# Layer 1's parts in another order, a softmax factor moved behind the product with the values, low parts of weights in pieces, and page arithmetic made earlier

## The chip, the core and the metric

The kernel runs on one core of a Trainium2 chip. The metric is the device time of one execution in microseconds (us), the median of several executions. Five engines of the core matter. TensorE (PE) multiplies; its operands are loaded by PEld rows. VectorE (DVE), ScalarE (ACT) and GpSimd (POOL) work on tiles. SyncE (SP), ACT's queue and POOL's queue issue DMA transfers. Each engine executes its own instructions in program order and waits for others by semaphores.

## What is computed

One inference step of a decoder with two layers, for a prompt of 512 tokens and 8 x 4 sample tokens, with the same weights. All matrices are float32; the width is 1024.

```python
for layer in range(DEPTH):
    hp = rms_norm(xp, norm_mix[layer])                 # and hs for the samples
    if layer % 2 == 0:                                 # HGRN2: gated linear recurrence, 6 heads
        tp, sp = hgrn2_mixer(hp @ w_in_hgrn, ...)
    else:                                              # DSA: 6 query heads, 2 key/value heads
        qp, kp, vp, iqp, ikp, iwp = dsa_project(hp @ w_in_dsa, ...)
        tp = dsa_prompt(qp, kp, vp, iqp, ikp, iwp)     # 128 keys chosen for each query by an index score
        ts = dsa_sample(...)                           # 256 of 1028, keys and values read by a page table
    cp = memory_attention(zp[..., -MEM_WIDTH:], ...)   # 4 heads into 256 memory tokens
    xp = xp + concat([tp, cp]) @ w_out[layer]
    xp = xp + conv_ffn(rms_norm(xp, norm_ffn[layer]), ...)

def gathered_attention(q, kg, vg, valid):
    s = einsum('btgrd,btkgd->btgrk', qg, kg) * D ** -0.5
    p = softmax(where(valid, s, -inf))                 # exp(s - max) / sum
    return einsum('btgrk,btkgd->btgrd', p, vg)
```

The outputs are the residual streams of both groups, the recurrent states, and the new keys and values.

## The kernel before

Activations lie feature-major, 128 features by 544 tokens (32 samples, then 512 prompt tokens). Every weight product is made of float32r parts: a weight block of 128x1024 (a unit) is loaded into raw, ACT casts it into whi, and DVE or POOL makes wlo = raw - whi; activations are split in hi and lo in the same way. A product is then three matmuls for each block: hi by whi, lo by whi, hi by wlo. 199 units are used in a fixed order.

The program is written out by a planner in Python. A main stream emits the products in order; beside it a Pump holds generators, each of which emits a few instructions of a head, a choice of keys or an attention per step and says on which tiles the step waits. A Model keeps a rough clock for each engine, and a step is given out when that clock says that its tiles are ready. Priorities (PRI, smaller first) and limits (KEEP, MAIN0, MAIN1, SLACK, BUSY, URGENT, MARGIN) decide among the steps. MIX orders the parts of layer 0: a number is a head of HGRN2 (its f and q products), hi two of its value products, g a gate product, mem the memory keys and values. ORDER does the same for layer 1: index (keys and queries of the index), q (one query head each), k, v, mq (memory queries), mkv, attn (which adds the attention's generators). All instructions are issued through one helper (L398 in the trace), so rows are told apart by tile names.

What the change and the prediction touch:

- Weights._cut (L740 to L762) casts a unit and makes its low part. The engine is chosen on the planner's clocks: DVE, if its clock is not later than that of PE and POOL plus a lead. The lead is LEAD0 = -1 in layer 0 and the MLPs, and LEAD1 = -100 in layer 1, so that there every low part goes to POOL, as one instruction of 1024 columns, about 21 of them.
- The page arithmetic (L1578 to L1592) stands after the output projection of layer 0: nine DMAs on ACT's queue load the page table in two forms (ptb, ptv), and DVE makes addresses of it (iidx, vidx). The next things on DVE are the sums and the factor of the following norm (tiles m__finish and rs), which PE spreads over the partitions (rb__finish).
- proj_tm makes a token-major product; for the samples it adds hi and lo of the 32 sample columns (eight POOL adds into sam) at each call, five calls in all.
- choose_sample finds the 256th largest score of a sample token bit by bit. A digit is a chain on DVE, ACT and PE: small integer instructions of 128x7 set seven thresholds, three counts of 128x264 run on DVE and four on ACT, and PE sums them (tile ple_choose_sample). One digit goes with one q product in the order of the program.
- choose_prompt takes the 128 largest scores of a query tile in 16 rounds; a round is MAX8 and MATCH_REPLACE8 on 256, 384 or 512 columns of isc. sbias and isc then mask the scores.
- prompt_attn (L1940) goes, for each head and query tile, from the scores (as) through exp (p, with its row sum su) to the transposes (apt, pt) and the product with the values (ao). scale_rows(p, su) multiplies p by 1/su on DVE or ACT before the transposes. In the last product the values are stationary, so ao is feature-major and is copied to outs[hd]; joined(hd) splits all 544 columns of it when the samples are there too.
- out_proj takes the heads in the order LAST.

```python
late = max(model.t["pe"], model.t["pool"]) + self.lead
(V if model.t["dve"] <= late else G).tensor_sub(lo[:, c:c + n], raw[:, c:c + n], hi[:, c:c + n].bitcast(F32))
```

## Time and profile before

| | |
|---|---|
| median of 3 runs | 1513.89 us (1504.01, 1513.89, 1514.38) |
| the profiled execution's span | 1500.7 us, mean granted clock 0.978 |
| PE busy | 1434.9 us (96%), 11314 matmuls |
| PEld, DVE, ACT, POOL busy | 1345.6, 803.2, 587.5, 567.3 us |
| DMA | 152.5 MB, mean 102 GB/s |
| chain that ended last | PE 84%, DVE 11%, issue 2%, ACT 1%, DMA 1% |

A share of busy time is a mean over stages with different limits; the granted clock is that of PE, 1.00 being its full rate. Layer 0's mixer runs to about 286 us, its output projection to 340, its MLP to 748; layer 1's mixer from 748 to 1049, then its output projection and MLP to the end. In a row of the timeline the bracket tells how long the engine was idle before the instruction, and what ended that idle time.

### The profile page before, as it was taken

How to read it: one execution, taken by the hardware profiler on the slowest of the kernel's cores; microseconds unless marked ns; L12 is line 12 of the kernel's file. 1: busy time of each engine (PE TensorE's matmuls, PEld its weight loads, DVE VectorE, ACT ScalarE, POOL GpSimd, SP SyncE). 2: the span in 40 equal slices, each digit the busy share in tenths (PEclk: the TensorE clock that was granted, in tenths of full speed). 3: DMA queues.
4: the chain of work that ended last, by engine and by line, in shares of the span. 5: the costliest groups of instructions: out<-in, count | busy, mean ns of one | idle time of the engine just before them, and what ended most of it. 6: DMA issues, size and time to landing. Idle time of an engine off the chain costs nothing.

```text
span 1500.7 us, 28191 instructions
## 1 busy us (share of the span) xinstructions
PE 1434.9 (96%) x11314; PEld 1345.6 (90%) x11314; DVE 803.2 (54%) x1762; ACT 587.5 (39%) x1064; POOL 567.3 (38%) x600
## 2 busy tenths in 40 slices
PE   8989999998999999999999797689999999999998
PEld 7978889998999999999987775456999999999998
DVE  7466886653444234444469988867444442244431
ACT  5447466332333123333335443466333331133320
POOL 4422444323444124446753444341134440144410
PEclk9999999999999999999999997989999999999999
DMA  5542132321333223224414236631222323232241
GB/s 186 177 156 64 59 117 86 101 85 62 88 95 93 92 73 94 90 85 126 135 54 131 83 115 202 199 127 57 71 76 89 96 85 99 73 95 87 85 121 57
DMA packets 60145, 152.52 MB, mean 102 GB/s; under 512 B 9040, under 2 KB 22960, under 8 KB 60016
## 3 DMA queue, kind: packets, MB, share of 16 engines
q1 hardware_dynamic: 39456, 110.11, 23.9%
q0 software_dynamic: 8208, 26.50, 5.4%
q10 hardware_dynamic: 12352, 14.13, 2.9%
q8 instruction: 89, 1.46, 0.4%
q14 instruction: 40, 0.33, 0.1%
HBM read 142.23 MB, written 8.47 MB: 100 GB/s over the span
## 4 chain that ended last, share of the span: by engine, by line
PE 84%; DVE 11%; issue 2%; ACT 1%; DMA 1%; another core or an unknown queue 0%; ACTq 0%; POOL 0%; SPq 0%; DVEq 0%; POOLq 0%
PE a L398 71%; DVE ple_choose_sample L398 2%; PE u_hgrn_head L398 1%; DVE isc_index_prompt L398 1%; PE id_index_prompt L398 1%; PE mkv L398 1%; PE ao_prompt_attn L398 1%; PE ho_hgrn_head L398 1%; PE ms_prompt L398 1%; PE hgrn_head_samples L398 1%; PE as_prompt_attn L398 1%; DVE t L398 1%; DMA ptv<-pt 1%; DVE lo L398 1%; PE mo_prompt L398 1%
## 5 line engine op out<-in xcount | busy, mean ns | idle before, releaser
L398 PE MATMUL a<-hi,whi 128*128 128x272 f32 x2640 | 556.4, 292 | 1.4 <-DVE t L398 1.0
L398 PE MATMUL a<-lo,whi 128*128 128x272 f32 x2640 | 551.0, 290 | 4.9 <-DVE lo L398 4.6
L398 POOL TENSOR_TENSOR wlo<-raw,whi 128x1024 fp32r<-128x1024 f32 x143 | 342.7, 2397 | 557.3 <-ACT whi L398 551.1
L398 PE MATMUL a<-hi,wlo 128*128 128x272 f32 x2640 | 549.1, 289 | 0.0
L398 PEld LDWEIGHTS a<-hi,whi 128*128 128x128 f32 x2640 | 417.7, 190 | 9.2 <-issue 5.4
L398 PEld LDWEIGHTS a<-lo,whi 128*128 128x128 f32 x2640 | 418.1, 190 | 6.2 <-DVE lo L398 5.6
L398 PEld LDWEIGHTS a<-hi,wlo 128*128 128x128 f32 x2640 | 418.1, 190 | 0.0
L398 ACT ACTIVATE whi<-raw 128x1024 fp32r<-128x1024 f32 (+1 forms) x202 | 209.5, 1038 | 230.9 <-PE a L398 151.3
L398 DVE TENSOR_TENSOR wlo<-raw,whi 128x1024 fp32r<-128x1024 f32 (+1 forms) x59 | 79.7, 1351 | 160.6 <-ACT whi L398 157.7
L398 DVE TENSOR_TENSOR sc<-a,rb 128x544 f32<-128x544 f32 x53 | 38.4, 724 | 116.1 <-PE a L398 114.5
L398 DVE SCALAR_TENSOR_TENSOR conv<-ext,params,conv 128x560 f32<-128x560 f32 x88 | 70.6, 802 | 45.1 <-ACT conv L398 43.6
L398 DVE TENSOR_TENSOR ext<-a,rb 128x240 f32<-128x240 f32 x132 | 37.5, 339 | 105.9 <-PE a L398 102.2
L398 ACT ACTIVATE conv<-ext,params 128x560 f32<-128x560 f32 x44 | 37.6, 855 | 136.2 <-DVE ext L398 132.6
L398 ACT ACTIVATE hi<-sc 128x544 fp32r<-128x544 f32 x44 | 29.0, 658 | 137.3 <-DVE sc L398 137.3
L398 DVE TENSOR_TENSOR x<-a,x 128x544 f32<-128x544 f32 x48 | 34.7, 723 | 80.1 <-PE a L398 72.5
L398 POOL TENSOR_TENSOR sqa<-sqa,sq 128x544 f32<-128x544 f32 x24 | 34.8, 1448 | 110.0 <-ACT sq L398 108.3
L398 DVE TENSOR_TENSOR sc<-sc,conv 128x512 f32<-128x512 f32 x88 | 62.5, 748 | 4.9 <-DVE sc L398 0.5
L398 ACT ACTIVATE conv<-conv 128x560 f32<-128x560 f32 x44 | 29.6, 672 | 73.8 <-DVE conv L398 73.8
L398 ACT ACTIVATE hi<-x,params 128x544 fp32r<-128x544 f32 x32 | 23.9, 745 | 70.4 <-DVE x L398 68.5
L398 DVE TENSOR_TENSOR lo<-sc,hi 128x544 fp32r<-128x544 f32 x44 | 31.9, 725 | 31.9 <-ACT hi L398 31.9
L398 PE MATMUL a<-whi,hi 128*128 128x256 f32 x160 | 46.8, 293 | 0.0
L398 PE MATMUL a<-whi,lo 128*128 128x256 f32 x160 | 45.1, 282 | 0.0
(406 smaller groups left out, 1931.9 us busy)
## 6 DMA issues: line engine op xcount, KB each, us to landing
raw<-w SPq DMA_DIRECT2D x177, 512.0 KB, 3.6
raw<-w POOLq DMA_DIRECT2D x21, 512.0 KB
k_sample_scores<-ckT SPq DMA_DIRECT2D x46, 128.0 KB, 3.5
ck_mem_samples<-cmkT ACTq DMA_DIRECT2D x16, 256.0 KB, 6.2
cv_mem_samples<-cmv ACTq DMA_DIRECT2D x16, 256.0 KB, 4.7
st_s<-hgrn_head_samples POOLq DMA_DIRECT2D x12, 256.0 KB
hgrn_head_samples<-hst SPq DMA_DIRECT2D x10, 256.0 KB, 3.5
ck_sample_scores<-ckT SPq DMA_DIRECT2D x18, 128.0 KB, 2.1
```

Source lines behind the costliest of these rows:

```text
L398: return f(*args, **kw)
```

## The change

It has six parts.

1. Order: MIX, ORDER and all of PRI, KEEP, MAIN0, MAIN1, SLACK, BUSY, URGENT, WAIT, MARGIN and PACE have other values, and the planner's costs know of PE's change between tile shapes and of the port that DVE and POOL share.
2. Low parts in layer 1: LEAD1 is -1, and what goes to POOL there is cut in pieces of 256 columns. By the order of the instructions, of the 21 low parts of this stage 12 are now on DVE and 9 on POOL, in four pieces each.
3. The factor 1/su is applied by ACT's copy of ao, no longer to p. So that it is a factor of rows, pt is now stationary, and ao comes out token-major; four transposes a head (aot) and a split bring it back. joined then splits only 32 sample columns. The samples' factor moves in the same way to their outputs.
4. Page arithmetic: the nine loads are issued before layer 0's heads, the addresses are made before its output projection.
5. sam is made once a layer (samples_of): 16 small POOL adds in place of 40.
6. Comments are gone.

```diff
-KEEP, MAIN0, MAIN1 = 3, 5, 1
+KEEP, MAIN0, MAIN1 = 0, 1, 5
-LEAD0, LEAD1, POOLED = -1.0, -100.0, 0
-WAIT, URGENT, EARLY = 1, 0.4, 0.4
+LEAD0, LEAD1, POOLED = -1.0, -1.0, 0
+PIECE = 256
+WAIT, URGENT, EARLY = 0, 0.2, 0.4
-PRI = dict(qsc=2, ip=2, isa=3, keys=3, sc=4, qsq=7, attn=5, sat=0, ...)
+PRI = dict(qsc=7.7, ip=5.5, isa=5.9, keys=7.5, sc=7.9, qsq=7.9, attn=6, sat=4.1, ...)
-MIX = "0 hi hi mem 1 2 3 4 hi 5 g g g g g g".split()
-ORDER = "index mem v q q q mem q q mem q k attn mq mkv".split()
+MIX = "0 hi hi mem g 1 2 3 4 g 5 hi g g g g".split()
+ORDER = "index q mem q mem q q q q k v mem attn mq mkv".split()
...
-                (V if model.t["dve"] <= late else G).tensor_sub(lo[:, c:c + n], raw[:, c:c + n], hi[:, c:c + n].bitcast(F32))
+                on, step = (V, n) if model.t["dve"] <= late else (G, self.piece)
+                for at in range(c, c + n, step):
+                    on.tensor_sub(lo[:, at:at + step], raw[:, at:at + step], hi[:, at:at + step].bitcast(F32))
...
+    ptb = cp.tile([128, 64], I32, name="ptb")
+    S.dma_start(ptb, bass.AP(tensor=pt_ap.tensor, offset=pt_ap.offset, ap=[[0, 128], [1, 64]]))
+    ptv = cp.tile([128, 8], I32, name="ptv")
+    for s in range(8):
+        S.dma_start(ptv[16 * s:16 * s + 16, :], bass.AP(tensor=pt_ap.tensor, offset=pt_ap.offset + s, ap=[[0, 16], [8, 8]]))
     memraw = []
...
-            scale_rows(p[:, :n], su)
-            yield [p]
...
-                T.matmul(ob[:, 0:128], vtok[k // 2][:, 256 * (k % 2) + 128 * g:256 * (k % 2) + 128 * g + 128],
-                         pt[:, 128 * k:128 * k + 128], start=k == 0, stop=k == tq)
-            S.activation(outs[hd][:, NS + 128 * tq:NS + 128 * tq + 128], ob[:, 0:128], AF.Copy)
+                T.matmul(ob[:, 0:128], pt[:, 128 * k:128 * k + 128],
+                         vtok[k // 2][:, 256 * (k % 2) + 128 * g:256 * (k % 2) + 128 * g + 128],
+                         start=k == 0, stop=k == tq)
+            S.activation(ot[:, 128 * tq:128 * tq + 128], ob[:, 0:128], AF.Copy, scale=su)
+        yield [ot]
+        tb = bank("aot")
+        for tq in range(4):
+            T.transpose(tb[:, 128 * tq:128 * tq + 128], ot[:, 128 * tq:128 * tq + 128], ident)
+        cat[hd] = pair()
+        yield from split2(tb, cat[hd], slice(NS, NT))
...
-        scale_rows(p, ri)
...
+        V.tensor_scalar(o[:, :256], o[:, :256], ri, None, op0=ALU.mult)
         yield [o]
```

Where the instructions now stand is decided by the planner. The first place is DVE's queue around the page arithmetic; before, it stands between the last square sum of the output projection (sqa) and the chain of the next norm's factor (m__finish).

```order
L398 TENSOR_TENSOR sqa_3520<-sqa_3520,sq_4038 128x544
L398 TENSOR_SCALAR iidx<-ptb,consts_81 64x32 x2
L398 TENSOR_SCALAR vidx<-ptv,consts_81 128x8
L398 TENSOR_SCALAR vidx<-vidx 128x8 x3
L398 TENSOR_SCALAR m__finish_1_4120<-st__finish_1_4111 128x5
L398 TENSOR_SCALAR m__finish_2_4122<-m__finish_1_4120 128x5
L398 TENSOR_SCALAR rs_4066<-m__finish_2_4122 128x5
```

In the changed kernel it stands between the last products of layer 0's heads (sc, on) and the split of a gated head (lo_gate):

```order
L404 TENSOR_TENSOR sc_3319<-sc_3319,on_hgrn_head_1_3447 128x544
L404 TENSOR_TENSOR sc_3474<-a_3328,rb_310 128x544
L404 TENSOR_SCALAR iidx<-ptb,consts_81 64x32 x2
L404 TENSOR_SCALAR vidx<-ptv,consts_81 128x8
L404 TENSOR_SCALAR vidx<-vidx 128x8 x3
L404 TENSOR_TENSOR lo_gate_1_3517<-sc_3319,hi_gate_1_3516 128x544
L404 TENSOR_SCALAR m_hgrn_head_2_3527<-m_hgrn_head_1_3028 128x5
```

The wait for ptv has moved ahead of the output projection, to a place where ptv was issued long before, and no longer stands ahead of m__finish.

The second place is DVE's queue in one q product of layer 1, before. rq and t are the rotation of a query head, ple_choose_sample (here by its longer names, _sample_choose_sample) is one digit.

```order
L398 SCALAR_TENSOR_TENSOR rq_9394<-a_9265,params_79,tab_9116 128x544
L398 SCALAR_TENSOR_TENSOR t_6_9395<-a_9265,params_79,tab_9118 64x544 x2
L398 TENSOR_SCALAR _sample_choose_sample_2_9032<-_sample_choose_sample_3_9440,_sample_choose_sample_2_9032 128x7
L398 TENSOR_SCALAR _sample_choose_sample_1_9031<-_sample_choose_sample_2_9032 128x1
L398 TENSOR_TENSOR _sample_choose_sample_1_9031<-_sample_choose_sample_1_9031 128x7
L398 TENSOR_TENSOR _sample_choose_sample_1_9031<-_sample_choose_sample_1_9031 128x1
L398 TENSOR_TENSOR _sample_choose_sample_1_9031<-consts_81,_sample_choose_sample_1_9031 128x7
L398 TENSOR_SCALAR _sample_choose_sample_1_9036,_sample_choose_sample_4_9034<-row_index_sample_3_9027,_sample_choose_sample_1_9031,_sample_choose_sample_2_9032 128x264 x3
```

The same place in the changed kernel; the whole of raw, whi and wlo is one weight unit:

```order
L404 SCALAR_TENSOR_TENSOR rq_9350<-a_9281,params_79,tab_8742 128x544
L404 SCALAR_TENSOR_TENSOR t_7_9351<-a_9281,params_79,tab_8744 64x544 x2
L404 TENSOR_TENSOR wlo_9357<-raw_8750,whi_9356 128x1024
L404 TENSOR_SCALAR _sample_choose_sample_2_9152<-_sample_choose_sample_3_9387,_sample_choose_sample_2_9152 128x7
L404 TENSOR_SCALAR _sample_choose_sample_1_9151<-_sample_choose_sample_2_9152 128x1
L404 TENSOR_TENSOR _sample_choose_sample_1_9151<-_sample_choose_sample_1_9151 128x7
L404 TENSOR_TENSOR _sample_choose_sample_1_9151<-_sample_choose_sample_1_9151 128x1
L404 TENSOR_TENSOR _sample_choose_sample_1_9151<-consts_81,_sample_choose_sample_1_9151 128x7
L404 TENSOR_SCALAR _sample_choose_sample_1_9156,_sample_choose_sample_4_9154<-row_index_sample_3_9146,_sample_choose_sample_1_9151,_sample_choose_sample_2_9152 128x264 x3
```

A low part of 1024 columns has come in between the rotation and the digit. On POOL, where before each q product had an rq add, a wlo and a load, there are now only the rq add and the load. Counted in the same rows, 23 rounds of the prompt's choice (MATCH_REPLACE) stand ahead of sbias before, and 12 in the changed kernel; the last round of the last tile is row 1178 of DVE's queue before and row 1160 now. The first q product now stands ahead of the first digit.

The third place is PE's queue at the end of the attention, before: the last heads' products with the values, and the first products of the output projection (a, with a joined head).

```order
L398 MATMUL ao_prompt_attn_4_12176<-pt_prompt_attn_4_12157,v_9113 128x128 x2
L398 MATMUL apt_prompt_attn_4_12186<-consts_80,p_prompt_attn_4_12064 128x128 x4
L398 MATMUL ao_prompt_attn_4_12193<-pt_prompt_attn_4_12174,v_9110 128x128 x2
L398 MATMUL ao_prompt_attn_4_12193<-pt_prompt_attn_4_12174,v_9113 128x128 x2
L398 MATMUL mpt_prompt_3_12203<-consts_80,mp_prompt_2_11996 128x128 x4
L398 MATMUL ao_prompt_attn_4_12210<-pt_prompt_attn_4_12191,v_9110 128x128 x2
L398 MATMUL ao_prompt_attn_4_12210<-pt_prompt_attn_4_12191,v_9113 128x128 x2
L398 MATMUL mot_join_1_12220<-consts_80,mo_mem_samples_1_10771 128x128 x4
L398 MATMUL mo_prompt_1_12226<-mpt_prompt_2_11985,mv_11194 64x256 x2
L398 MATMUL mo_prompt_1_12226<-mpt_prompt_4_12208,mv_11194 64x256 x2
L398 MATMUL a_11327<-hi_joined_1_12200,whi_10839 128x272 x2
```

In the changed kernel (hi_prompt is the memory attention's part of the input, hi_prompt_attn a head's):

```order
L404 MATMUL ao_prompt_attn_4_12218<-v_10259,pt_prompt_attn_4_12203 128x128 x2
L404 MATMUL ao_prompt_attn_4_12218<-v_10262,pt_prompt_attn_4_12203 128x128 x2
L404 MATMUL apt_prompt_attn_3_12225<-consts_80,p_prompt_attn_3_12184 128x128 x3
L404 MATMUL a_11363<-hi_prompt_1_11753,whi_11079 128x272 x2
L404 MATMUL a_11363<-lo_prompt_1_11754,whi_11079 128x272 x2
L404 MATMUL a_11363<-hi_prompt_1_11753,wlo_11080 128x272 x2
L404 MATMUL aot_prompt_attn_1_12237<-consts_80,ct_prompt_attn_1_10871 128x128 x4
L404 MATMUL ao_prompt_attn_3_12245<-v_10259,pt_prompt_attn_3_12229 128x128 x2
L404 MATMUL ao_prompt_attn_3_12245<-v_10262,pt_prompt_attn_3_12229 128x128
L404 MATMUL as_prompt_attn_4_12250<-kT_9880,rq_9600 128x512
L404 MATMUL a_11362<-hi_prompt_attn_1_12030,whi_11079 128x272 x2
```

Products of the output projection now stand between the last heads' parts, and each head has its transposes (aot) behind its product with the values.

## Rows read from the trace of the kernel before

**Rows 1.** The page: its first line.
```profile
span 1500.7 us, 28191 instructions
```

**Rows 2.** Windows: from:to, length, busy us (instructions) of PE, PEld, DVE, ACT, POOL; clock, DMA.
```profile
1200.00:1300.00 100.00, 100.00 (x799) 100.00 (x799) 31.49 (x43) 23.93 (x26) 23.69 (x22) 1.00 0.31 91
```

**Rows 3.** Windows, the same columns, of the stages of layer 1.
```profile
748.00:778.00 30.00, 26.38 (x213) 25.67 (x214) 23.80 (x56) 6.25 (x9) 19.08 (x23) 0.99 0.22 65
778.00:870.00 92.00, 82.58 (x580) 70.20 (x580) 79.76 (x190) 50.02 (x129) 37.85 (x47) 0.95 0.29 90
870.00:912.00 42.00, 37.12 (x319) 32.06 (x318) 35.05 (x125) 20.77 (x49) 22.39 (x31) 0.94 0.49 151
912.00:976.00 64.00, 44.05 (x309) 28.57 (x309) 52.57 (x182) 25.09 (x72) 23.54 (x22) 0.82 0.64 205
976.00:1049.00 73.00, 67.05 (x441) 42.86 (x441) 51.95 (x156) 48.04 (x138) 22.83 (x24) 0.91 0.28 93
```

**Rows 4.** Timeline of DVE (start, duration, instruction, [idle before <-releaser]), 336 to 358.
```profile
349.65 0.23 DVE L398 TENSOR_SCALAR vidx<-ptv,consts 128x8 int32<-128x8 int32 x1 [10.00 <-DMA ptv<-pt]
...
352.35 0.17 DVE L398 SCALAR_TENSOR_TENSOR rs<-m__finish,rs 128x5 f32<-128x5 f32 x1
```

**Rows 5.** Timeline of PE, 338 to 354: the sums and the factor.
```profile
339.41 1.12 PE L398 MATMUL st__finish<-consts,sqa 128*128 128x1 f32 x16
...
352.57 1.36 PE L398 MATMUL rb__finish<-consts,rs 128*128 128x128 f32 x5 [5.05 <-DVE rs L398]
```

**Rows 6.** Windows, columns as above, after the wait.
```profile
353.00:359.00 6.00, 6.00 (x33) 5.54 (x32) 3.53 (x7) 2.21 (x4) 0.32 (x2) 0.64 0.00 0
```

**Rows 7.** Timeline of ACT and its queue (ACTq), 20 to 36 and 336 to 342.
```profile
33.79 0.69 ACT L398 ACTIVATE rb<-rb__finish 128x512 f32<-128x512 f32 x2 [5.24 <-PE rb__finish L398]
...
336.76 3.35 ACTq L398 DMA_DIRECT2D ptv<-pt  x7
```

**Rows 8.** Timeline of PE, 84 to 104: waits for a head.
```profile
90.27 0.63 PE L398 MATMUL ot_hgrn_head<-consts,o_hgrn_head 128*128 128x128 f32 x4 [1.50 <-DVE o_hgrn_head L398]
92.47 0.41 PE L398 MATMUL ots_hgrn_head<-consts,oss_hgrn_head 128*128 128x32 f32 x2 [1.57 <-DVE oss_hgrn_head L398]
```

**Rows 9.** Groups of POOL, 748 to 1049: sample columns.
```profile
L398 POOL TENSOR_TENSOR sam<-hi,lo 128x32 f32<-128x32 f32 x16 | 4.2, 296 | 0.1
```

**Rows 10.** Timeline of POOL, 846 to 862: one q product.
```profile
856.49 1.35 POOL L398 TENSOR_TENSOR rq<-rq,t 128x544 f32<-128x544 f32 x1 [7.92 <-DVE t L398]
857.81 2.38 POOL L398 TENSOR_TENSOR wlo<-raw,whi 128x1024 fp32r<-128x1024 f32 x1
```

**Rows 11.** Timeline of DVE, 846 to 866: the same q product.
```profile
850.95 0.17 DVE L398 TENSOR_TENSOR ple_choose_sample<-consts,ple_choose_sample 128x7 int32<-128x7 int32 x1
...
856.88 1.05 DVE L398 TENSOR_TENSOR ple_choose_sample<-ple_choose_sample 128x7 int32<-128x7 int32 x2
857.97 2.25 DVE L398 TENSOR_TENSOR ple_choose_sample<-consts,ple_choose_sample 128x7 int32<-128x7 int32 x1
...
864.65 1.02 DVE L398 TENSOR_TENSOR ple_choose_sample<-ple_choose_sample 128x7 int32<-128x7 int32 x2
```

**Rows 12.** Tile wlo, DVE, 1100 to 1500: count, ns min/median/max, first and last start.
```profile
L398 DVE TENSOR_TENSOR wlo<-raw,whi x14: 1224/1226/1227, 1238.8 to 1479.6; 128x1024 fp32r<-128x1024 f32 x14
```

**Rows 13.** Groups of DVE by shape, 748 to 1049: count, busy us, mean ns, idle before.
```profile
L398 DVE MATCH_REPLACE8 isc_index_prompt<-mpt_choose_prompt,isc_index_prompt 128x384 f32<-128x384 f32 x16 | 8.7, 543 | 0.0
...
L398 DVE TENSOR_SCALAR qss<-qss 128x30 f32<-128x30 f32 x2 | 3.0, 1518 | 0.0
```

**Rows 14.** The same, shapes together, and one of them in the timeline.
```profile
L398 DVE TENSOR_SCALAR p_prompt_attn<-p_prompt_attn,m_prompt_attn 128x512 f32<-128x512 f32 (+3 forms) x14 | 10.2, 726 | 0.5
...
962.86 3.18 DVE L398 TENSOR_SCALAR p_prompt_attn<-p_prompt_attn,m_prompt_attn 128x256 f32<-128x256 f32 x1
```

**Rows 15.** Timeline of PE, 966 to 1036: transposes of p, last scores.
```profile
971.29 0.60 PE L398 MATMUL apt_prompt_attn<-consts,p_prompt_attn 128*128 128x128 f32 x4
...
1030.30 5.42 PE L398 MATMUL as_prompt_attn<-kT,rq 128*128 128x512 f32 x12
```

81 lines of the change are left out of this document (46 added, 35 removed).

## Prediction

> **What bounds the kernel now.** I read the time in three steps: the page for the whole, the windows for the stages in which TensorE (PE) loses time, then the timelines of those stages for what it waits on. The profiled execution spans 1500.7 us [rows 1]. PE is the bound: over most of the program it is busy for the whole of a window at a granted clock of 1.00, as from 1200 to 1300, where 799 matmuls of a product take 100 us, 0.125 us each [rows 2]. There nothing in this change can help, since the products stay. So I count lost time: a stage's idle time plus its busy time x (1 - clock). In layer 1's mixer that is 3.9 us (748 to 778, index), 13.5 (778 to 870, scores, selection, q products), 7.1 (870 to 912), 27.9 (912 to 976, memory keys and first heads) and 12.0 (976 to 1049, the other heads), together 64 us of 301 [rows 3]. From 778 to 912 it is VectorE (DVE) that is busy, 79.8 of 92 and 35.1 of 42 us [rows 3]. The reader should see stages in which PE waits for DVE again and again and runs at a lower clock after the waits. Outside layer 1 the largest loss is one wait near 348, below.
>
> **The page arithmetic.** DVE's queue stands still for 10.00 us before vidx until ptv has landed. The factor's chain stands behind it and ends at 352.52, and PE's rb has then waited 5.05 us [rows 4, 5]. After it the clock is 0.64 over 6 us, a further 6 x 0.36 = 2.2 us [rows 6]. In the changed order the nine loads are issued some 300 us earlier, and vidx stands before the output projection, so the chain can start when PE's sums end, at 340.53. Next late would be the chain itself: with vidx it takes 352.52 - 349.65 = 2.9 us, and PE had products until 347.52, 7 us after its sums [rows 4, 5]; they hide it. Gain 7.2 us. The nine issues now lie on ScalarE's (ACT's) queue at about 27 us, behind the layer's first products; seven took 3.35 us, so nine take about 4.3. ACT idles 5.24 us there, ahead of rb [rows 7], which covers them; what is queued behind them is a weight's cast and rb, and without the cover they would cost up to 4 us. I take 0.
>
> **Layer 0's order, sample columns.** Before, PE waits 1.50 and 1.57 us for a head's output [rows 8]; now 24 more products stand ahead of such transposes, and the gate products between the heads. But the last head ends nearer to the output projection and can wait there as the first did. I take -2, between -3.1 (both waits gone) and +3.1 (both come again at the end). The 24 POOL adds left out take 0.3 us each [rows 9], on an engine with much idle time there: 0.
>
> **Low parts in layer 1.** A digit's period on DVE is 864.65 - 856.88 = 7.8 us. In it one instruction of 128x7, which takes 0.17 us when POOL is idle, takes 2.25: it starts at 857.97, and POOL's low part lasts from 857.81 to 860.19 [rows 10, 11]. Two others take 1.05 together beside POOL's rq add, which stays. The changed order has no low part on POOL in the q products, so 2.25 - 0.17 = 2.1 us go per digit; in return DVE makes the low part, 1.23 us when nothing disturbs it [rows 12]. That is -0.9 for each of four digits with a low part among them and -2.1 for three without: -10. But a q product is 48 matmuls of 0.125 us [rows 2], 6 us, and with the digit's own small products a period can't fall much below 6.5; I count -6. The two scalings of qss, 30 columns, mean 1.52 us [rows 13], have the same stall: -2.6. In the index stage five low parts go to DVE, 5 x 1.23 = 6.2 us, for stalls of a like size; with the first q product there as other work for PE I take -2, between 0 and -3.9, all that is lost [rows 3].
>
> **Rounds put off.** By DVE's order 11 rounds of the prompt's choice move from before sbias to behind it. The replacement of 384 columns is 0.54 us [rows 13], the search I take as long, and some have 256 columns: 1 us a round, 11 us. In 778 to 912, where 20.6 us are lost, I let their absence give a third, -3.4. With the -8.6 that is -12, between 0 (the low parts on DVE eat it) and -20.6 (PE full).
>
> **The attention.** Fourteen scalings of p leave DVE, 10.2 us at a mean of 0.73, and ten leave ACT; 1/su now rides on a copy that ACT makes anyway. The longest took 3.18 us, 256 columns beside a whole low part [rows 14]; a piece of 256 is a quarter of 2.38 [rows 10], 0.6 us or somewhat more. Of stalls of 2 us or more on other instructions I count four, -8. Added on DVE are 11 us of rounds and two low parts, 2.5; on PE 24 transposes at 0.60 for four, +3.6 [rows 15]. DVE: -10.2 - 8 + 11 + 2.5 = -4.7. The heads also come staggered: before, the twelve last scores came together at 1030.30 [rows 15] and every head ended after them; now output products run between the last heads. At each head's end there are new waits (copy, transposes, split), and the next head's products are queued behind them; the output products between, some 30 pairs, 7.5 us, cover them. I take -5, between -20 (half of the 40 us lost) and +14 (rounds and transposes alone).
>
> **Sum.** -7.2 - 2 - 2 - 12 - 5 = -28 us, against a profiled span of 1500.7 us. The nearest timed run is 1504.0, so 3.3 us lie around it; the median is 1513.9, 10 above that run for no reason that the rows show. I take the sum off the median: 1486.
>
> **Rivals.**
> 1. DVE's relief reaches PE nearly in full: two thirds of layer 1's 64 us go, -41, with the page wait -48: 1466. For it speaks DVE's busy share in the lost stages; against it, that the rounds come back and that the clock stays low for some us after each wait that is left. Chance 0.15.
> 2. Only the page wait and layer 0 count, -9: 1505. What the q products gain is given back in the attention, since 16 rounds for the last tile gate the last scores in both orders, and 11 more rounds stand before them. For it: the last scores start right where DVE's rounds end, at 1030.30 [rows 15]. Against it: DVE sheds more there than it takes. Chance 0.18.
> 3. The pieces stop DVE as often as a whole low part did: DVE runs one instruction between two pieces and waits for the next, four waits of 0.6 us or more for one of 2.4. Then the -8 of the attention doesn't come: -20, 1494. Against it: many of DVE's instructions there read PSUM or have one input. Chance 0.14.
> 4. The other side, slower. DVE is the bound of 778 to 912 and has no room for low parts: 12 x 1.23 = 14.8 us lie on its path, with 11 of rounds and 3.6 of transposes, while the stalls that go were in time that it would have waited anyway: -7.2 - 2 + 14.8 + 11 + 3.6 = +20, 1534. It is slower as soon as less than 20 us of stalls and scalings go in all of layer 1, of the 31 that I counted (10 + 2.6 + 10.2 + 8). Against it: the stall of 2.25 us lies in series with the rest of the digit [rows 11]. Chance 0.07.
> 5. The change doesn't do what it says: ptv lands late again at its new place. It would take 300 us for what took 10; no chance of its own.
>
> The Trainium skill (SBUF — State Buffer, "Who interferes with whom") says that the engine that starts first keeps the pair of ports shared by DVE and POOL for its whole instruction, and that the other blocks fully. By that rule each piece can stop an instruction, which is rival 3, 1494. This trace agrees on whole low parts, where the stalled instruction ended 0.03 us after POOL's; no row shows pieces.
>
> **Numbers.** My forecast has a chance of 0.46 and a range of its own from 1478 to 1496. Under 1%, 15 us, is about what a measurement of this kernel can't tell from no change. Faster are the forecast, rival 1 and most of rival 3: 0.72. The same are rival 2 and the rest of rival 3: 0.21. Slower is rival 4: 0.07. The range, 1466 to 1508, leaves out rival 4 and half of rival 1.
>
> **What would show it.** No idle time before vidx, no wait of PE before rb there, the clock at 1.00 from 340 to 360. In the q products the 128x7 instruction at 0.2 us, DVE's low parts at 1.2, a digit's period near 6.7. In the attention no scaling of p, 24 transposes at 0.15 us, and PE's lost time from the memory keys to the output projection near 35 us instead of 40. I am wrong if the time lost there grows, if DVE's low parts take 2 us, or if PE waits at the last head for longer than its output products cover.

## The result: 1.2% slower, on the other side of the forecast

The changed kernel takes 1526.1 us (median of four runs, 1525.0 to 1529.4) against 1510.0 for the kernel before: a ratio of 1.0118, with a 95% interval from 1.0083 to 1.0152. The forecast was 1486 us in a range from 1466 to 1508, so the time lies above the range and on the other side. The page of the changed kernel, first line, against [rows 1]:

```profile
span 1524.7 us, 28256 instructions
```

The spans differ by 24.0 us where the medians differ by 16.1, since the execution of the kernel before that was profiled ran some 8 us below the median of its runs. To see where the 24 us came from I cut both executions at the four places where PE makes a norm's sums (tile st__finish). The last column runs to the end.

| us | layer 0's mixer and output projection | its feed-forward part | layer 1's mixer and output projection | its feed-forward part |
|---|---|---|---|---|
| before | 339.4 | 407.6 | 354.8 | 398.9 |
| changed | 361.2 | 399.9 | 363.6 | 400.0 |
| difference | +21.8 | -7.7 | +8.8 | +1.1 |

One term of the sum came as forecast, the page arithmetic. DVE of the changed kernel, timeline as in [rows 4]: vidx no longer waits, and the factor's chain starts with the sums. PE's wait of [rows 5] and the low clock of [rows 6] are gone: from the sums on, PE is busy for the whole of 25 us at a clock of 1.00 (the window below, with the columns of [rows 3]).

```profile
309.25 0.23 DVE L404 TENSOR_SCALAR vidx<-ptv,consts 128x8 int32<-128x8 int32 x1
...
362.46 0.17 DVE L404 TENSOR_SCALAR m__finish<-st__finish 128x5 f32<-128x5 f32 x1 [1.35 <-PE st__finish L404]
```

```profile
361.00:386.00 25.00, 25.00 (x206) 24.68 (x205) 11.98 (x31) 7.37 (x10) 10.45 (x12) 1.00 0.22 65
```

Layer 0, for which -2 was forecast, lost 21.8 us. Its idle time plus the excess of its time at the lower clock, summed over windows of 2 us up to the start of the output projection (286 us before, 306 after), is 16 us before and 34 after; what is left, the work at full clock, is about the same, 270 and 272 us. PE's timeline in the changed kernel has new waits beside those of [rows 8], for ACT's cast of the memory and late in the mixer for DVE:

```profile
93.97 0.80 PE L404 MATMUL mkv<-whi,hi 128*128 128x512 f32 x1 [2.38 <-ACT hi L404]
...
245.01 0.66 PE L404 MATMUL ot_hgrn_head<-consts,o_hgrn_head 128*128 128x128 f32 x4 [2.39 <-DVE o_hgrn_head L404]
...
280.91 0.49 PE L404 MATMUL ho_hgrn_head<-v,sct 128*128 128x128 f32 x2 [2.75 <-DVE hgrn_head_samples L404]
```

Layer 1's stages, windows with the columns of [rows 3]. By the same count of lost time the index stage went from 3.9 us to nothing, from the scores to the memory keys 20.6 became 26.1 (the second to fourth line), and the attention's 39.9 became 49.3 (the last two).

```profile
762.00:782.00 20.00, 20.00 (x167) 19.76 (x167) 14.72 (x41) 4.67 (x7) 10.82 (x19) 1.00 0.39 123
782.00:822.00 40.00, 39.50 (x267) 29.45 (x266) 32.81 (x64) 23.81 (x56) 15.94 (x34) 1.00 0.36 107
822.00:908.00 86.00, 74.00 (x563) 65.76 (x562) 66.58 (x217) 39.59 (x108) 26.23 (x29) 0.86 0.24 74
908.00:936.00 28.00, 26.41 (x205) 22.19 (x205) 22.81 (x91) 11.22 (x22) 13.03 (x23) 0.94 0.75 236
936.00:1000.00 64.00, 42.21 (x307) 25.00 (x306) 42.87 (x153) 26.68 (x73) 30.65 (x35) 0.79 0.63 203
1000.00:1064.00 64.00, 52.20 (x327) 32.42 (x327) 41.97 (x134) 36.86 (x115) 12.44 (x14) 0.87 0.19 61
```

The digits, DVE's timeline, against [rows 11]. The instruction of 128x7 takes 0.17 us, as forecast, and DVE's low part 1.23. But the period is 852.91 - 844.30 = 8.6 us, not 6.5.

```profile
844.30 0.17 DVE L404 TENSOR_TENSOR ple_choose_sample<-consts,ple_choose_sample 128x7 int32<-128x7 int32 x1
...
847.93 0.79 DVE L404 SCALAR_TENSOR_TENSOR rq<-a,params,tab 128x544 f32<-128x544 f32 x1 [1.81 <-ACT qsq L404]
...
850.34 1.23 DVE L404 TENSOR_TENSOR wlo<-raw,whi 128x1024 fp32r<-128x1024 f32 x1
...
852.91 0.17 DVE L404 TENSOR_TENSOR ple_choose_sample<-consts,ple_choose_sample 128x7 int32<-128x7 int32 x1
```

DVE waits 1.81 us for ACT, which counts four thresholds and makes qsq; the stall of 2.25 us before (857.97 to 860.22) had lain beside these counts, as ACT's timeline of the kernel before shows, where qsq follows them:

```profile
857.96 0.52 ACT L398 ACTIVATE ple_choose_sample<-row_index_sample,ple_choose_sample 128x264 f32<-128x264 f32 x1 [3.02 <-DVE ple_choose_sample L398]
...
860.40 0.60 ACT L398 ACTIVATE qsq<-a 128x544 f32<-128x544 f32 x1
```

The low part is in series. POOL's timeline of the changed kernel shows its addition, 1.35 us in [rows 10], beside it:

```profile
850.40 2.38 POOL L404 TENSOR_TENSOR rq<-rq,t 128x544 f32<-128x544 f32 x1 [5.71 <-DVE t L404]
```

From the first digit to the ninth, the starts of ACT's counts are 60.6 us apart before (829.98 to 890.56) and 59.2 after (836.24 to 895.47): a gain of 1.4 us in all.

### The profile page after: what moved, and what is told of

Same layout as the page of the kernel before. It is cut to its first block, busy times and chain, and to the rows that moved or that the text cites. A ratio compares the mean times of both kernels' runs of the same rounds, so it can differ in the third digit from the quotient of the medians.

```text
span 1524.7 us, 28256 instructions
## 1 busy us (share of the span) xinstructions
PE 1449.1 (95%) x11338; PEld 1351.3 (89%) x11338; DVE 803.2 (53%) x1765; ACT 586.7 (38%) x1062; POOL 544.3 (36%) x588
## 4 chain that ended last, share of the span: by engine, by line
PE 78%; DVE 9%; ACT 2%; issue 2%; DMA 1%; SPq 0%; ACTq 0%; DVEq 0%
PE a L404 67%; PE ms_prompt L404 1%; PE u_hgrn_head L404 1%; PE id_index_prompt L404 1%; DVE isc_index_prompt L404 1%; DVE m_hgrn_head L404 1%; PE ao_prompt_attn L404 1%; DVE wlo L404 1%; DVE ple_choose_sample L404 1%; ACT ple_choose_sample L404 1%; DVE sc L404 1%; DMA k_sample_scores<-ckT 1%; PE ho_hgrn_head L404 1%; PE as_prompt_attn L404 1%; PE mkv L404 1%
## 5 line engine op out<-in xcount | busy, mean ns | idle before, releaser
L404 POOL TENSOR_TENSOR wlo<-raw,whi 128x1024 fp32r<-128x1024 f32 (+1 forms) x156 | 316.1, 2033 | 605.0 <-ACT whi L404 605.0
L404 DVE TENSOR_TENSOR wlo<-raw,whi 128x1024 fp32r<-128x1024 f32 (+1 forms) x73 | 99.4, 1361 | 161.8 <-ACT whi L404 155.6
```

The lines of the kernel that those rows point to most:

```text
L404: return f(*args, **kw)
```

## Experiments

The kernel before ran beside every group on the same chip; its median was 1513.2 (e1 to e4), 1493.8 (e5 to e8, and e9 to e12), 1511.3 (e13 to e16) and 1510.4 us (e17, e18). So times are compared by ratios to it. "Settings" are the planner's constants (PRI, KEEP, MAIN0, MAIN1, PACE, WAIT, URGENT, SLACK, BUSY, MARGIN, its costs) with MIX or ORDER. The table has the stages of each profiled execution, and for layer 1's mixer the end of tile 3's choice of keys (DVE's last instruction on isc) and what follows it.

| | ratio, 95% interval | layer 0 | feed-forward 0 | layer 1 | of it to the choice's end | rest |
|---|---|---|---|---|---|---|
| before (first profile) | 1 | 339.4 | 407.6 | 354.8 | 283.3 | 71.5 |
| changed (first profile) | 1.0118, 1.0083 to 1.0152 | 361.2 | 399.9 | 363.6 | 279.0 | 84.6 |
| e1 old settings, layer 0 | 1.0028, 1.0009 to 1.0046 | 351.3 | 399.0 | 369.9 | 282.8 | 87.1 |
| e2 old settings, layer 1 | 1.0222, 1.0186 to 1.0259 | 360.5 | 400.3 | 385.4 | 311.7 | 73.6 |
| e3 old settings, both | 1.0169, 1.0138 to 1.0199 | 351.8 | 399.6 | 385.3 | 312.5 | 72.9 |
| e4 low parts on POOL | 1.0148, 1.0120 to 1.0176 | 356.7 | 400.1 | 370.6 | 286.0 | 84.6 |
| e5 before + page | 1.0021, 1.0006 to 1.0036 | 352.9 | 400.6 | 343.1 | 271.2 | 71.9 |
| e6 before + sample columns | 1.0075, 1.0051 to 1.0099 | 341.5 | 407.4 | 352.7 | 280.0 | 72.7 |
| e7 before + factor | 1.0068, 1.0042 to 1.0094 | 341.5 | 407.4 | 351.3 | 269.5 | 81.8 |
| e8 before + low parts | 1.0136, 1.0105 to 1.0168 | 342.3 | 407.2 | 360.1 | 290.8 | 69.3 |
| e9 attention's rank | 1.0124, 1.0094 to 1.0154 | 359.5 | 399.3 | 353.0 | 260.4 | 92.7 |
| e10 page loads by SP | 0.9958, 0.9943 to 0.9973 | 343.5 | 400.4 | 342.3 | 270.4 | 71.9 |
| e11 e8, low parts on POOL | 1.0130, 1.0100 to 1.0160 | 342.4 | 407.0 | 359.9 | 291.0 | 69.0 |
| e12 combined | 0.9972, 0.9954 to 0.9990 | 340.5 | 399.7 | 347.8 | 256.7 | 91.1 |
| e13 changed, again | 1.0087, 1.0053 to 1.0122 | 362.8 | 399.5 | 361.1 | 276.5 | 84.6 |
| e14 e12, rank 6 | 1.0031, 1.0010 to 1.0053 | 341.4 | 400.7 | 366.3 | 281.1 | 85.3 |
| e15 e12, no factor | 1.0143, 1.0121 to 1.0166 | 342.7 | 400.3 | 384.7 | 276.1 | 108.6 |
| e16 e12, values early | 1.0007, 0.9982 to 1.0033 | 343.5 | 400.3 | 358.5 | 278.5 | 80.1 |
| e17 page loads by ACT | 0.9954, 0.9938 to 0.9971 | 343.5 | 401.0 | 359.0 | 287.5 | 71.5 |
| e18 changed, loads by SP | 1.0114, 1.0092 to 1.0136 | 360.8 | 404.0 | 362.7 | 278.0 | 84.7 |

### e1 to e3: the settings undone

```diff
 e1: layer 0, e2: layer 1's mixer, e3: both
-PACE, KEEP, MAIN0, MAIN1 = 2.0, 0, 1, 5         (and the rest as the change has it)
+PACE, KEEP, MAIN0, MAIN1 = 1.0, 3, 5, 1         (and the rest, MIX and ORDER as before)
```

> The changed kernel with the planner's settings and the mix of the products of before in layer 0 alone (page arithmetic and sample columns stay early, layer 1 as changed). Theory A, that layer 0's new order costs the 18 us by which its mixer's lost time (TensorE's idle time and its time at half clock) grew from 16 to 34 us: layer 0's output projection begins near 288 instead of 305.8, and the time is near 1508, about that of the kernel before. Rival B, that layer 0 lost through the page loads that now stand in ScalarE's queue and the sample columns made early: the projection still begins past 300 and the time stays near 1526.

> The changed kernel with the planner's settings and the order of the products of before in layer 1's mixer alone (the factor moved, low parts in pieces or on VectorE, as the change has them). Theory A, that layer 1's new order is worth its 8.8 us loss: the mixer from st to st takes some 355 instead of 363.6 us and the time is near 1517. Rival C, that the code (factor at the outputs, low parts on VectorE) is what costs: the mixer stays near 363 and the time near 1526. My recorded terms (selection -12, attention -5 from factor, ports and low parts) would give 340 and 1502.

> Settings, mix and order of before in both layers, with all of the change's code (early page arithmetic, early sample columns, factor at the outputs, low parts by the new rule). Theory A: 1503 from the page arithmetic (-7) with nothing else gained, or less by what the factor brings, at the lowest 1490. Rival C, that the code costs: 1510 or more.

e1 gives half of an answer: layer 0's mixer falls from 361.2 to 351.3 us, not to 340. On the same chip, e2 and e4, with the changed order in layer 0, have 360.5 and 356.7. So the new settings cost it 5 to 10 us, and some 12 more come from something that e1 kept. (Layer 1 comes out in another order too, though its settings are those of the change: thirteen score tiles stand behind the choice there, not twelve.) e2 falls out on the far side of all that was expected: with the order of before, layer 1's mixer is not 355 or 363 but 385.4 us, and the ratio 1.0222. So the change's code is worse off with the settings of before (1.0222 against 1.0118). This code, put under the order rules of before, takes 26 us more than the longest that this mixer took with the code of before (359.0 in e17). e3 repeats both: 351.8 and 385.3.

### e4: the low parts on POOL, in the changed order

```diff
     on, step = (V, n) if model.t["dve"] <= late else (G, self.piece)
+    if on is V and self.queue is G: on = VG      # POOL, booked on the planner's clock of DVE: the order stays
```

> The changed kernel, instruction for instruction, with the 12 low parts of layer 1's mixer that VectorE made on GpSimd instead, whole. Theory D, that the low part's 1.23 us lies in series in the choice's digits while the port stall that went had lain beside ScalarE's counts: the digits' period falls from 8.6 and 8.05 to about 7.8, and the time falls by 1 to 4 us. The recorded step (a port stall of 2.1 us per digit comes back): the period goes to 9.5 and the time rises by 6 to 10 us.

The starts of nine digits' counts are 58.5 us apart (839.27 to 897.81) against 59.2 in the changed kernel, although the stall is back in three of them, as in this one:

```profile
846.29 2.25 DVE L404 TENSOR_TENSOR ple_choose_sample<-consts,ple_choose_sample 128x7 int32<-128x7 int32 x1
```

So in the digits it is worth little which engine makes the low parts: the stall has room there. But the time does not fall, against theory D. The ratio, 1.0148, is 3 parts in a thousand above the 1.0118 and 6 above the 1.0087 of e13, with intervals that overlap, and layer 1's mixer, 370.6 us, is 7 to 10 us longer than in three executions of the changed order (363.6, 361.1 in e13, 362.7 in e18). That loss lies ahead of the digits, where neither expectation looked: at the start of layer 1, in the chain of the norm's factor. One of its instructions of 128x5 takes 3.11 us beside POOL's pieces of a low part (762.04 to 764.79), and PE waits for rb. DVE's and PE's timelines of e4:

```profile
761.71 3.11 DVE L404 SCALAR_TENSOR_TENSOR rs<-m__finish,rs 128x5 f32<-128x5 f32 x1
...
765.48 1.19 PE L404 MATMUL rb__finish<-consts,rs 128*128 128x128 f32 x5 [3.43 <-DVE rs L404]
```

In the changed kernel no link of this chain takes longer than 0.23 us, and PE does not wait there. In e4 the choice for tile 1, 2 and 3 then ends 6, 7 and 7 us later, counted from the mixer's start.

### e5 to e8: one part of the change at a time, on the kernel before

```diff
 e5:  +loads of ptb, ptv ahead of the parts of MIX in layer 0 (ACT's queue); +iidx, vidx ahead of out_proj(0)
 e6:  +samples_of(h) once a layer, at its start; -eight additions at each proj_tm
 e7:  -scale_rows(p, su)   +S.activation(ot, ob, AF.Copy, scale=su)   +four transposes (aot) and split2 for each head
 e8:  -LEAD1 = -100.0      +LEAD1 = -1.0, PIECE = 256
```

> The kernel before with the early page loads and page arithmetic alone. Layer 1's first wait after layer 0's output projection goes: the stage from the norm's sums ahead of layer 0's feed-forward part to those behind it falls from 407.6 to 400 us (as it did in every run that had this edit), and nothing else moves: -7 us. Rival: the nine loads in ScalarE's queue during layer 0's mixer hold back what stands behind them there, and the mixer gives the gain back: 0.

> The kernel before with the sample columns alone made early, in both layers. My recorded step priced it at nothing. Rival, from e1 and e3, whose layer 0 under the settings of before still came to its norm's sums at 351.5 us instead of 339.4: early sample columns move work on GpSimd and the planner's choices after it, and layer 0 loses 8 to 12 us: +8 to +12 in the whole.

> The kernel before with the softmax factor alone moved to the attention's outputs; TensorE's order is that of before up to the choice's last stretch. My recorded terms for this part give -4 to -7 (14 scalings by 0.73 to 3.18 us less, transposes 3.6 us more). Rival C, from e3, whose attention lost 30 us more than that of before: the outputs' transposes and splits, which begin only when a head's four tiles are done, put new waits on TensorE and half-clock stretches behind them: +15 to +30.

> The kernel before with the rule for low parts alone (VectorE where it is not late, else GpSimd in pieces of 256 columns) in layer 1's mixer. My recorded terms give -6 to -10 (port stalls of VectorE gone, low parts added). Theory D, low parts in series with the choice's digits: 0 to +5. Rival C in the form that the low parts are what cost the 30 us of e3: +15 or more.

None of the four pays alone. e5 has its 7 us in the feed-forward part (407 to 400.6) and gives 10 back in layer 0's mixer. e6 is not dear in layer 0, where it was looked for, but in layer 1: the choice's end moves from 271.2 (e5, whose layer 1 is that of before, on the same chip) to 280.0 us. It is the wait of e4 again. The eight additions into sam now stand on POOL at the start of the layer with a low part behind them, one instruction of the factor's chain takes 4.02 us beside the two, and PE waits for rb, as it does not in e5. POOL's, DVE's and PE's timelines of e6:

```profile
751.63 1.72 POOL L398 TENSOR_TENSOR sam<-hi,lo 128x32 f32<-128x32 f32 x8
753.32 2.33 POOL L398 TENSOR_TENSOR wlo<-raw,whi 128x1024 fp32r<-128x1024 f32 x1
...
751.65 4.02 DVE L398 TENSOR_TENSOR m__finish<-rs 128x5 f32<-128x5 f32 x1
...
756.73 1.36 PE L398 MATMUL rb__finish<-consts,rs 128*128 128x128 f32 x5 [3.57 <-DVE rs L398]
```

The granted clock is 0.76 in the 13 us behind this wait. e7 leaves the choice's end where it was and lengthens the rest from 71.9 to 81.8: the samples' last product with the values comes at 293.5 us of the mixer instead of 279.2. e8 ends the samples' choice 8.9 us earlier (its last product at 158.4 us against 167.3 in e5), more than the 6 us that I had forecast for the digits, and the choice of tile 3 some 20 us later.

### e10, e17 and e18: the page loads, with the order held

```diff
 e10: +nc.sync.dma_start(ptb, ...), eight of ptv, ahead of out_proj(0); the planner books them where they were
 e17: +nc.scalar.dma_start(ptb, ...), eight of ptv, where e5 has them; the planner books them where they were
 e18: the changed kernel; -loads in layer 0's mixer, +loads as in e10, +iidx, vidx behind out_proj(0); booked as in the change
```

> The kernel before with its nine page loads issued by SyncE ahead of layer 0's output projection instead of by ScalarE behind it; the arithmetic stays where it was and every other engine's order is that of before. Theory F, that e5 gained 7 us at the page wait and lost them in layer 0's mixer only because of where its loads stood in ScalarE's queue and what the planner made of them: here the wait of 10 us on the page table goes, layer 0's mixer keeps its 340 us, and the ratio is 0.995 to 0.996 (-6 to -8 us). Rival: the norm's sums behind the feed-forward part or the mixers give it back: 1.000.

> The kernel before with its nine page loads in ScalarE's queue at the place where e5 has them (behind the first memory queries, near 27 us), the arithmetic where it was, and every engine's order as in the kernel before. e5 lost 10 us of layer 0's mixer against e10. Theory J, that ScalarE's 4 us for nine issues, which hold back the weight cast behind them (31.61 us in e5, 27.50 before), are that loss: layer 0's norm sums come near 350 us and the ratio is 1.000 to 1.003. Rival K, that the loss came from the order that the planner then made (state loads ahead of a weight in SyncE's queue, casts later): here they come at 340 to 344 us and the ratio is 0.995 to 0.997, as in e10.

> The changed kernel, each engine's order held, with its nine page loads issued by SyncE ahead of layer 0's output projection as in e10, and the seven page instructions on VectorE behind that projection. Theory J: layer 0's sums come at 352 to 356 us instead of 361 to 363, and the ratio falls to 1.003 to 1.007. Rival K: they stay at 358 to 363 us and the ratio at 1.009 to 1.012, so that what layer 0 lost is in its order.

In e10 SP issues the loads at 287 us, as the row of tile ptv shows (count, ns, first and last start):

```profile
L1585 SPq DMA_DIRECT2D ptv<-pt x8: 424/428/430, 287.4 to 290.7; - x8
```

In DVE's timeline of e10 vidx then stands right in front of the chain, without a wait:

```profile
345.22 0.23 DVE L403 TENSOR_SCALAR vidx<-ptv,consts 128x8 int32<-128x8 int32 x1
```

The ratio is 0.9958, 6 us of the 7 that I forecast. e17 has the nine loads where e5 had them. In ACT's timeline the cast of a weight waits 3.40 us for their issue, as it does in e5, yet layer 0's mixer is 343.5 us and the ratio 0.9954.

```profile
31.30 1.06 ACT L403 ACTIVATE whi<-raw 128x1024 fp32r<-128x1024 f32 x1 [3.40 <-DMA ptv<-pt]
```

So the 4 us on ACT's queue cost nothing that the ratio shows, as I had it, and the 10 us that e5 lost come from the order that the planner makes once it knows of the loads. One of its marks is in SP's queue, where in e5 a weight's load stands behind two loads of states, at 70.92:

```profile
60.49 0.33 SPq L398 DMA_DIRECT2D raw<-w  x1
68.89 1.14 SPq L398 DMA_DIRECT2D _hgrn_head_samples<-hst  x2
70.92 4.30 SPq L398 DMA_DIRECT2D raw<-w  x2
```

In e17, as before, it stands ahead of them, at 64.98:

```profile
64.98 0.33 SPq L403 DMA_DIRECT2D raw<-w  x1
67.46 2.42 SPq L403 DMA_DIRECT2D _hgrn_head_samples<-hst  x2
```

The other is on PE, whose timeline in e5 has waits for ACT that e17 and e10 have not:

```profile
81.10 2.08 PE L398 MATMUL u_hgrn_head<-v,km_hgrn_head 128*128 128x128 f32 x8 [2.67 <-ACT oss_hgrn_head L398]
...
99.79 0.79 PE L398 MATMUL mkv<-whi,hi 128*128 128x512 f32 x1 [3.32 <-ACT hi L398]
```

Which of these differences costs how much was not separated. e18 takes loads and arithmetic out of the changed kernel's layer 0 and keeps its order: 360.8 us and 1.0114, no change. Layer 0's loss is in its order. (Its feed-forward part is 404.0 us: vidx then stood in front of the factor's chain, one link of the chain took 2.22 us, and PE waited 2.30 us for rb.) PE's timeline of e18 has a long wait for a head, and late in the mixer the one shown above:

```profile
102.30 0.63 PE L409 MATMUL ot_hgrn_head<-consts,o_hgrn_head 128*128 128x128 f32 x4 [4.03 <-DVE o_hgrn_head L409]
...
280.69 0.52 PE L409 MATMUL ho_hgrn_head<-v,sct 128*128 128x128 f32 x2 [2.75 <-DVE hgrn_head_samples L409]
```

e17 and e18 ran on one chip, so their 25 us can be split without a change of chip: 17.3 us in layer 0, 3.1 in its feed-forward part, 3.7 in layer 1 and 0.9 behind it. Most of what the change loses is lost in layer 0.

### e11: DVE's time, or the order

```diff
 e8, order held:
+    if on is V and self.queue is G: on = VG
```

> The kernel of e8, instruction for instruction, with the 13 low parts that VectorE made in layer 1 on GpSimd instead. In e8 tile 3's choice of keys on VectorE ended at 290.8 us from the mixer's start, against 271.2 in e5, which has layer 1 as before, on the same chip. Theory G, that VectorE's own time up to that end is the bound, and the 13 low parts (1.23 us each, 16 us) go into it: the choice ends 12 to 16 us earlier and the ratio falls from 1.0136 to about 1.004. Rival H, that the order in which the planner put the rounds of the choice is what made them late: the end stays near 290 and the ratio above 1.01.

Thirteen low parts, 16 us, leave DVE, and the choice ends at the same place, 1040.32 - 749.5 = 290.8 us from the mixer's start in e8 and 1040.36 - 749.4 = 291.0 in e11. DVE's timeline of e8, the last instruction of the choice:

```profile
1040.32 0.43 DVE L399 TENSOR_SCALAR isc_index_prompt<-isc_index_prompt 128x512 f32<-128x512 f32 x1
```

And that of e11:

```profile
1040.36 0.43 DVE L399 TENSOR_SCALAR isc_index_prompt<-isc_index_prompt 128x512 f32<-128x512 f32 x1
```

This speaks for H and against G, and with it against my rival 4, by which the low parts would lie on DVE's path. The order itself shows what moved: of the 48 rounds of the choice, 23 stand ahead of sbias in DVE's queue in e5, as in the kernel before, and 7 in e8 and in e11.

### e9, e12 to e16: the rest after the choice

In every run with the rules of before in layer 1 and without the moved factor, the rest after the choice is 69 to 73 us, wherever the choice ends; with the factor moved under the rules of before it is 73 to 82 (e2, e3, e7); with the change's rules and its factor it is 80 to 93, and 109 without the factor (e15). DVE's program order shows one difference. Below, each figure is a score tile (0 to 3) of a head, in order; a bar is the end of the choice for tile 1, 2 and 3.

```
before   000000|111111|222222|333333
changed  000000|1111|22|331223132323
e9       000000|111111|222222|333333
e14      000000|1111|2|2213213332233
```

In the changed kernel twelve score tiles stand behind the last bar. DVE's timeline there, with the choice's end first and some of the score tiles (128x256 is tile 1, 128x512 tile 3), the last of them 34 us later:

```profile
1040.11 0.43 DVE L404 TENSOR_SCALAR isc_index_prompt<-isc_index_prompt 128x512 f32<-128x512 f32 x1
...
1045.46 0.40 DVE L404 CUSTOM_DVE_ANT_0 p_prompt_attn<-as_prompt_attn,isc_index_prompt 128x256 f32<-128x256 f32 x1
...
1054.74 0.42 DVE L404 CUSTOM_DVE_ANT_0 p_prompt_attn<-as_prompt_attn,isc_index_prompt 128x256 f32<-128x256 f32 x1
...
1074.05 0.69 DVE L404 CUSTOM_DVE_ANT_0 p_prompt_attn<-as_prompt_attn,isc_index_prompt 128x512 f32<-128x512 f32 x1 [3.96 <-PE as_prompt_attn L404]
```

In e10, with the order of before, DVE has six behind it, all of tile 3, within 6 us:

```profile
1014.32 0.43 DVE L403 TENSOR_SCALAR isc_index_prompt<-isc_index_prompt 128x512 f32<-128x512 f32 x1
1015.88 0.69 DVE L403 CUSTOM_DVE_ANT_0 p_prompt_attn<-as_prompt_attn,isc_index_prompt 128x512 f32<-128x512 f32 x1 [1.14 <-PE as_prompt_attn L403]
...
1020.36 0.69 DVE L403 CUSTOM_DVE_ANT_0 p_prompt_attn<-as_prompt_attn,isc_index_prompt 128x512 f32<-128x512 f32 x1
```

```diff
 e9, the changed kernel (e13 is the changed kernel with nothing edited):
-PRI = dict(..., attn=6, ...)
+PRI = dict(..., attn=3.5, ...)
 e12: layer 0 in the order of before, page loads as in e10, layer 1 as changed, and the edit of e9
 e14, on e12:
-attn=3.5
+attn=6
 e15, on e12:
+scale_rows(p, su)                                       (and p, ri of the samples)
-S.activation(ot, ob, AF.Copy, scale=su), aot, split2    (a plain copy, joined as before)
 e16, on e12:
-sat=4.1, val=4.5
+sat=3, val=3
```

> The changed kernel with the rank of the prompt attention among the generators raised (6 becomes 3.5), nothing else. In the changed kernel 12 of the 24 score tiles of the prompt attention (six heads, four tiles each) stand behind the end of tile 3's choice of keys, in the kernel before 6 do: the six of tile 3. With the rank raised it is 6 again. Theory E, that the attention's end hangs on what is left behind that choice: the last score tile comes 5 to 10 us behind the end of the choice instead of 33, layer 1's mixer falls by 10 to 20 us and the time is 1505 to 1515, ratio 0.995 to 1.005. Rival: the tail is bound by TensorE's work that is left (transposes, output products), and the time stays: ratio 1.01.

> Layer 0 in the order of the kernel before to the instruction (sample columns made at their use), the page loads as in e10, layer 1 with the change's settings, factor and low parts, and the attention's rank as in e9. If theories E and F hold, the page wait gives -7 and layer 1's mixer is no longer than before's by more than 3 us: ratio 0.990 to 0.998, the best of all. If the loss of layer 1 is in the moved factor itself (e7 lost 8 us with nearly before's order): 1.000 to 1.005.

> The changed kernel itself, on one chip with the runs beside it. e9, which differs from it in the attention's rank alone, came to a ratio of 1.012 on another chip, with layer 1's mixer of 353.0 us where the changed kernel's own profile shows 363.6. Theory E (what stands behind tile 3's choice sets the end): here the mixer is 8 to 15 us longer than in e9, the last score tile comes some 30 us behind the end of the choice, and the ratio is 1.015 to 1.02. Rival: the rank was worth nothing and the chips differ: the mixer is within 4 us of 353 and the ratio is 1.012.

> The kernel of e12 with the attention's rank of the change (6) in place of 3.5; TensorE's order is that of e12 up to the attention's second tile. Theory E: the heads fall behind one another again, some 12 score tiles stand behind tile 3's choice, and the ratio is 1.003 to 1.009 against 0.997 in e12. Rival: it stays at 0.997.

> The kernel of e12 with the softmax factor where the kernel before has it (on the exponentials, ahead of their transposes). If the moved factor costs 8 us, as e7 says of the settings of before: ratio near 0.992. If it pays under the settings of the change, by the scalings that VectorE and ScalarE are spared (my recorded term: -7): ratio 1.000 or more.

> The kernel of e12 with the ranks of the samples' attention and of its values raised too (4.1 and 4.5 become 3). In e12 the samples' values are the last thing ahead of the output projection (their last product at 291.4 us from the mixer's start, against 278.4 in e10). If they set the end: they finish near 275, layer 1's mixer falls from 347.8 to 340 and the ratio to 0.990 to 0.994. If the prompt's heads set it: the ratio stays at 0.997 or rises.

e9 is a miss for theory E in the time: 1.0124 against 1.0118 and 1.0087 (e13) for the changed kernel. The heads go abreast again, and the rest does not shrink: it grows from 84.6 to 92.7. (The choice ends 16 us earlier than in e13, but on another chip; in one and the same order its end moves by as much between e10 and e17.) DVE's timeline of e9, the choice's end and the last score tile, 21 us behind it:

```profile
1019.18 0.43 DVE L404 TENSOR_SCALAR isc_index_prompt<-isc_index_prompt 128x512 f32<-128x512 f32 x1
...
1040.48 0.69 DVE L404 CUSTOM_DVE_ANT_0 p_prompt_attn<-as_prompt_attn,isc_index_prompt 128x512 f32<-128x512 f32 x1 [0.30 <-PE as_prompt_attn L404]
```

Samples are late now. PE's timeline of e9: their second group's transposes wait for ACT 29 us after the choice's end.

```profile
1048.44 2.19 PE L404 MATMUL spt_sample_attn<-consts,sr 128*128 128x128 f32 x9 [2.38 <-ACT sr L404]
```

e12 and e14, which differ by the rank alone, are at 0.9972 and 1.0031, intervals apart, but on two chips. e16, on the chip of e14, has the raised rank and brings the samples' values forward as well (last product at 279.2 us instead of 291.4); heads fall behind again (eight score tiles behind the last bar), and its 1.0007 has an interval that overlaps that of e14. So it is not shown that the rank pays. All this would fit a rest that is set by whichever chain the ranks leave last, prompt heads or samples; no run took both in, and that cause stays open.

e15 is against what e7 seemed to say. Under the rules of before the moved factor costs 7 parts in a thousand; under those of the change its absence costs 17 against e12 on another chip (1.0143 against 0.9972), and 11 and 14 against e14 (1.0031) and e16 (1.0007) on its own, which differ from it in ranks too. One trace of it, in PE's timeline of e15, is a wait for p, which is scaled there ahead of its transposes:

```profile
929.88 0.45 PE L427 MATMUL apt_prompt_attn<-consts,p_prompt_attn 128*128 128x128 f32 x1 [7.59 <-DVE p_prompt_attn L427]
```

The factor has no price of its own here, since the planner's order changes with it in both comparisons.

## Why the prediction was wrong, step by step

- **Page arithmetic, -7.2.** Right in size and mechanism: -7.7 in the changed kernel, -6 to -7 in the whole when the rest of the order is held (e10, e17). Taking 0 for the nine issues on ACT was right too (e17). What I left out is that the planner sees them: the order that it then makes costs layer 0 10 us (e5).
- **Layer 0's order, -2, between -3.1 and +3.1.** The step that failed: +21.8, and +17.3 between e17 and e18 on one chip. I bounded it by the two waits of [rows 8], as if the new order could only remove or repeat them. Old settings give 5 to 10 us back (e1), the rest is the order that the planner makes with the page loads (e5, e17, e18). Which waits of the new order cost how much stays open. The nearest rows were no bound: they show what the old order waits for, and nothing of what a new one may.
- **Sample columns, 0.** Right for layer 0 (341.5 us in e6) and, as far as the trace shows, for the changed kernel. The reason that I gave, POOL's idle time, was not enough: put into the kernel before, the same edit cost layer 1 some 9 us (e6), because the additions and a low part fell beside the factor's chain and stopped DVE there for 4.02 us.
- **Index stage, -2.** Right in sign and about in size: the 3.9 us lost there went to nothing. The low parts on DVE matter here more than in the digits, since with them on POOL the factor's chain is stopped and PE waits (e4).
- **Digits, -6.** Mis-sized. Each row was read rightly (2.25 to 0.17, a low part of 1.23), but I counted seven digits with the stall where five of these nine have it (the 128x7 instruction takes 0.17 us at 850.95 in [rows 11] already), the stall lay beside ACT's counts, and the low part lies in series: -1.4 over nine digits. The samples' choice did end earlier, by 6 us from the mixer's start (165.1 to 159.0), since the digits begin earlier; PE's lost time did not fall with it. The Trainium skill (SBUF — State Buffer, "Who interferes with whom") says that the shared ports are held for a whole instruction by the engine that starts first. POOL's addition, 2.38 us beside DVE's low part against 1.35 before, agrees. Which of the two waits made no measurable difference in the digits (e4, e11); in the factor's chain, with nothing beside it to hide the wait, it did (e4, e6).
- **Scalings of qss, -2.6, and rounds put off, -3.4.** The two scalings fell from 3.0 to 1.3 us, not to 0.4. The rounds' absence shows in no relief: in the stage from which they went, PE's lost time grew from 20.6 to 26.1 us. (A third of the 11 us would have been -3.7.)
- **Attention, -5.** +13.1 in the rest after the choice (71.5 to 84.6, the same within 0.2 us in e4, e13 and e18), against -4.3 up to its end. I named the gate, tile 3's choice, in rival 2, and the staggered heads too, but took the products between them for a cover. They cover too little: PE's lost time there went from 39.9 to 49.3 us, and twelve score tiles wait behind a choice that six had waited for. That the stagger is the cause is not shown: e9 takes it away, and the rest grows.
- **Rivals.** Rival 4 has the right sign, by luck: e11 and e4 speak against its mechanism. Rival 3 was not tried by itself; POOL's pieces took 0.72 to 1.24 us each. In rival 1, two thirds of 64 us are 43, not 41. None of the five had layer 0's order as its mechanism, although part 1 of the change sets it anew.

## What to carry to other kernels

Where a planner writes the order, an edit has two prices: that of its instructions and that of the order made anew around it. Hold the order (emit the instruction elsewhere but book it where it was) to measure the first; here nine DMA issues moved that way gain 0.4%, the best of all runs (0.9958 and 0.9954), and the same edit left to the planner loses 0.2% (e5). Settings fitted to one code say little of another: each part of the change loses under the old settings, and the factor's absence loses under the new ones. The same stall of VectorE beside GpSimd cost next to nothing in a digit, where other work lay beside it, and made PE wait 3.4 to 3.6 us in the chain of a norm's factor (e4, e6): price a stall by what waits for the series it is in. And before pricing instructions in a stage, look for the event on which the rest hangs (here perhaps the end of tile 3's choice), count what stands behind it, and test it; taking the count back to six did not bring the time down (e9).

## What the runs showed of the chip

The kernel's layer 1 in the order of before took 342.3 us on one chip (e10) and 359.0 on another (e17), instruction for instruction; 354.8 in the first profile. Up to 225 us from its start the two are 3 us apart. Then, while POOL issues gathers, PE, DVE and ACT of e17 stand still together for some 5 us, for nothing that the profile shows. PE's timeline of e17:

```profile
977.20 0.66 PE L403 MATMUL apt_prompt_attn<-consts,p_prompt_attn 128*128 128x128 f32 x2 [4.80 <-issue]
```

ACT's:

```profile
977.83 0.62 ACT L403 ACTIVATE p_prompt_attn<-p_prompt_attn,m_prompt_attn 128x384 f32<-128x384 f32 x1 [6.41 <-issue]
```

And PE's of e10, where the same product waits 0.53 us:

```profile
970.70 0.55 PE L403 MATMUL apt_prompt_attn<-consts,p_prompt_attn 128*128 128x128 f32 x3 [0.53 <-ACT pt_prompt_attn L403]
```

The first profile of the kernel before has it too, and the changed kernel has one of 5.5 us on ACT up to 968.03. Its cause is open; no run was made for it. Behind it the difference grows: tile 3's choice ends 17 us later in e17 than in e10. A difference of 5 us between kernels is therefore read from ratios on one chip, not from two profiles of different ones.
